# Attention: row minima and the two parts of the turned exponentials get a higher scheduling priority

## The chip, the cores and the metric

One core of a Trainium2 chip runs the whole program. The metric is the device time of one execution in microseconds (us). The engines are TensorE (PE in the profile; its weight loads are PEld), VectorE (DVE), ScalarE (ACT), GpSimd (POOL) and SyncE (SP, which issues DMAs). Each works off its own list of instructions in order; an instruction that has to wait holds everything behind it on that engine.

## The reference, cut to what matters

The model has two layers, each with a feed-forward part, a mixer and another feed-forward part, for 512 tokens of width 1024. The first mixer is a gated short convolution, the second is sparse attention. The change lies in the attention alone:

```python
def masked_softmax(logits, valid):
    p = jax.nn.softmax(jnp.where(valid, logits, NEG_INF), axis=-1)
    return jnp.where(valid, p, 0.0)
...
p_c = masked_softmax(s_c, dist_c >= 0)                 # 31 compressed blocks
p_s = masked_softmax(s_s, (dist_s >= 0)[:, :, None])   # selected blocks
p_w = masked_softmax(s_w, valid_w)                     # window
out = gb[..., 0:1] * o_c + gb[..., 1:2] * o_s + gb[..., 2:3] * o_w
```

There are 16 heads in 4 groups of 4; the heads of a group share keys and values. With 512 tokens all 8 selectable blocks are chosen, so the selected and the window branch are both plain causal attention over all tokens, each with keys of its own.

## The kernel before, in words

Matrix products are made from split values: a number is kept as a rounded high part and the low part that is left (`split`, L174: ScalarE copies the high part, VectorE subtracts it), and a product is three matmuls (`mm3`, L178).

`attend` (L1007) computes the attention. Its work comes in 32 **units**, one for each group g, head q of the group and branch b: units 0 to 7 are group 0, 8 to 15 group 1, and so on (L1010). The 512 query rows of a unit are four blocks of 128; block i sees (i+1)x128 keys. A unit is worked in three steps c, with the blocks (3), (2, 0) and (1). Per step and unit:

- `logits` (L1074): TensorE multiplies queries and keys into a PSUM tile `s` (L1084; two buffers). Queries and keys are held as a high and a low half in one tile, and the keys in both orders, so two matmuls make a block.
- `smallest` (L1089): VectorE adds the bias table, writes the (negated) logits to `L` and takes the minimum of each row in the same instruction (L1094); the second row that the order and the trace show for it reads the accumulator. There are four for a unit, one for each block. `L` has three buffers.
- `exponentials` (L1099): ScalarE takes the exponentials in place and sums the rows (L1103).
- `scaled` (L1106): when all four blocks are there, VectorE takes the reciprocal of the sums (L1109) and GpSimd multiplies it by the gate (L1111) and scales the four blocks of `L` (L1114).
- `turn` (L1116): TensorE transposes the blocks of `L` into a PSUM tile `pt` (L1123; two buffers). ScalarE copies the high part `pth` (L1127), VectorE subtracts it for the low part `ptl` (L1129, returned as `low` and called later).
- `apply` (L1131): TensorE multiplies values by `pth` and `ptl` into `o` (L1140, L1141); `finish` (L1143) adds the compressed branch from `pch`, `pcl` when a head is done, and VectorE and ScalarE write `osum`, `ohi`, `olo`.

The loop at L1209 is a software pipeline written by hand: with LEAD = 3, turn v brings `logits` and `smallest` of unit v+3, `scaled` of v+2, `turn` of v+1 and `apply` of v. Between these stand pieces of other work (`fill`): the projections of values and queries of later groups (`value_steps`, `query_steps`: 12 matmuls a piece into `nat`), a root-mean-square norm of the new queries on VectorE (`normed` L782, whose ten small instructions are `rsqrt` L202), their transposes into heads and keys (`heads` L993, `keys` L982), the compressed branch (`compressed` L1032: matmuls `pc`, VectorE rows L1045 to L1059, transposes `pct`), the output projection of finished groups (`out_steps` L1164: six matmuls into `y`, then `yt` on ScalarE and an addition on GpSimd), and weights for what follows, which VectorE and ScalarE split (`weights` L183; `wlo`, `ehlo` on VectorE). After the loop the tail multiplies the last two groups (`ty`, L1246).

The order in which instructions stand on each engine is not that of the text. A scheduler sets it: each instruction has a priority, by its place in the text unless `tc.high_priority()` raises it, and for each engine the scheduler takes, of what it reckons to be ready, what has the highest priority. The kernel already raises the norms between layers in this way (L266, L286, L382), nothing within `attend`. All other parts of the program are the same before and after.

Of the kernel before, what the change touches and what calls it, by code (L numbers as in the profile page):

```python
# [16 lines left out]
AF = mybir.ActivationFunctionType  # L17
# [36 lines left out]
def decoder_kernel(ctx, tc, xT, cT, ng, adaw, adab, ffi, ffo, cwi, cw, cwo,  # L54
                   nwi, nwg, pos, w1, w2, qg, kg, nwo, rb, onehot, rowok, out):
    nc = tc.nc
# [20 lines left out]
    def psum(name, tag="mm"):  # L77
        tag = next(six) if tag == "mm" else {"pr": "o"}.get(tag, tag)
        return ps.tile([P, T], F32, name=name, tag=tag, bufs=2)
# [650 lines left out]
    def nsa(s, nrm, nxt, w0, ahead):  # L730
        with ExitStack() as es:
# [112 lines left out]
            with ExitStack() as es2:  # L844
# [31 lines left out]
                run(v1[1:])  # L876
                keys(0, 1)
            return attend(es, s, nxt, ahead, K, Q, keys, heads, vn, kch, kcl, vcc, gsb, query_steps, value_steps, last_weight, hpool)


# [126 lines left out]
    def attend(nsa_es, s, nxt, ahead, K, Q, keys, heads, vn, kch, kcl, vcc, gsb, query_steps, value_steps, last_weight, hpool):  # L1007
# [3 lines left out]
        with ExitStack() as es:  # L1011
# [8 lines left out]
            def table(g, q):  # L1020
                n = g * NG + q
                for e in range(P // NR):
                    src = bass.AP(tensor=tbl.tensor, offset=tbl.offset + n * NR * TBL + P - 1 - NR * e,
                                  ap=[[TBL - 1, NR], [1, T]])
                    nc.sync.dma_start(tb[NR * e:NR * (e + 1), q, :], src)
# [48 lines left out]
            def logits(u, c):  # L1074
                g, q, b = units[u]
                if c == 0:
                    Ls[u] = at.tile([P, 1280], F32, name="L", bufs=3)
                    sts[u] = sp.tile([P, 2 * NB], F32, name="st")
                sps = psum("s", "s")
                off = 0  # L1080
                for i in ((3,), (2, 0), (1,))[c]:
                    n = (i + 1) * P
                    for e, m in enumerate(K[b]):
                        nc.tensor.matmul(sps[:, off:off + n], Q[q][:, i * P:(i + 1) * P], m[:, 0:n],  # L1084
                                         start=(e == 0), stop=(e == 1))
                    off += n
                return sps

            def smallest(u, c, sps):  # L1089
                g, q, b = units[u]  # L1090
                off = 0
                for i in ((3,), (2, 0), (1,))[c]:
                    n = (i + 1) * P
                    nc.vector.tensor_tensor_reduce(out=Ls[u][:, LOFF[i]:LOFF[i] + n], in0=sps[:, off:off + n],  # L1094
                                                   in1=tb[:, q, T - n:T], scale=1.0, scalar=3e38,
                                                   op0=ALU.add, op1=ALU.min, accum_out=sts[u][:, i:i + 1])
                    off += n

            def exponentials(u, c):  # L1099
                st = sts[u]  # L1100
                for i in ((3,), (2, 0), (1,))[c]:
                    l = Ls[u][:, LOFF[i]:LOFF[i] + (i + 1) * P]
                    nc.scalar.activation(l, l, AF.Exp, bias=st[:, i:i + 1], scale=-1.0,  # L1103
                                         accum_out=st[:, NB + i:NB + i + 1])

            def scaled(u):  # L1106
                g, q, b = units[u]
                r = sp.tile([P, NB], F32, name="r")
                nc.vector.reciprocal(r, sts[u][:, NB:2 * NB])  # L1109
                f = sp.tile([P, NB], F32, name="f")  # L1110
                nc.gpsimd.tensor_tensor(f, r, gsb[:, :, (g * 4 + q) * 3 + 2 - b], ALU.mult)  # L1111
                for i in range(NB):
                    l = Ls[u][:, LOFF[i]:LOFF[i] + (i + 1) * P]
                    nc.gpsimd.tensor_scalar(l, l, f[:, i:i + 1], 0.0, op0=ALU.mult, op1=ALU.add)  # L1114

            def turn(u, c):  # L1116
                pt = psum("pt", "t")
                off, segs = 0, []
                for j in ((0,), (1, 3), (2,))[c]:
                    segs.append((j, off))  # L1120
                    for i in range(j, NB):
                        cc = LOFF[i] + j * P
                        nc.tensor.transpose(pt[:, off:off + P], Ls[u][:, cc:cc + P], ident)  # L1123
                        off += P
                hi = at.tile([P, off], F32R, name=f"pth{c}")
                lo = at.tile([P, off], F32R, name=f"ptl{c}")
                nc.scalar.activation(hi, pt[:, 0:off], AF.Copy)  # L1127
                pts[u, c] = hi, lo, segs
                return lambda: nc.vector.tensor_tensor(lo, pt[:, 0:off], hi, ALU.subtract)  # L1129

            def apply(u, c):  # L1131
                g, q, b = units[u]
                hi, lo, segs = pts.pop((u, c))
                if b == 0 and c == 0:
                    os[g, q] = psum("o", "o")
                o = os[g, q]
                for j, cc in segs:
                    n = T - j * P
                    v = vn[b][j][:, g].rearrange("p a e -> p (a e)")
                    nc.tensor.matmul(o[:, j * P:T], v, hi[:, cc:cc + n], start=(b == 0 and j == 0), stop=False)  # L1140
                    nc.tensor.matmul(o[:, j * P:T], v, lo[:, cc:cc + n], start=False, stop=False)  # L1141

            def finish(u):  # L1143
                g, q, b = units[u]
                if b == 0:
                    return
                o = os.pop((g, q))
                nc.tensor.matmul(o, vz[:, q, :], pch, start=False, stop=False)
                nc.tensor.matmul(o, vz[:, q, :], pcl, start=False, stop=True)
                e = q % 2  # L1150
                if e == 0:
                    os["sum"] = at.tile([P, T], F32, name="osum")
                osum = os["sum"]
                mine, other = slice(e * HD, (e + 1) * HD), slice((1 - e) * HD, (2 - e) * HD)
                nc.scalar.activation(osum[mine], o[other], AF.Copy)
                nc.vector.tensor_tensor(osum[mine], o[mine], osum[mine], ALU.add)
                if e == 1:
                    hi, lo = [(tp if g % 2 else ow).tile([P, T], F32R, name=n, tag="t", bufs=4) for n in ("ohi", "olo")]
                    split(osum, hi, lo)
                    oh.append(hi)  # L1160
                    ol.append(lo)
# [17 lines left out]
            LEAD, N = 3, len(units)  # L1179
# [3 lines left out]
            for g in range(NG):  # L1183
                v0 = 8 * g
                c = compressed(g)
# [16 lines left out]
            def share(v):  # L1202
                for steps, v0, v1 in shares:
                    if v0 <= v < v1:
                        n = 11
                        return steps, n * (v - v0 + 1) // (v1 - v0) - n * (v - v0) // (v1 - v0), v == v1 - 1
                return None, 0, False

            for v in range(START, N):  # L1209
                a, b, u = v + LEAD, v + 1, v  # L1210
                steps, n, end = share(v)
                todo = needed[v] + [lambda: next(steps, None)] * n

                def fill(left):
                    for _ in range(-(-len(todo) // left)):
                        todo.pop(0)()

                for c in range(3):
                    if 0 <= u:
                        apply(u, c)  # L1220
                        if c == 2:
                            finish(u)
                    if 0 <= a < N:
                        sps = logits(a, c)
                    if c == 0 and 0 <= a - 1 < N:
                        scaled(a - 1)
                    if 0 <= b < N:
                        low = turn(b, c)
                    if 0 <= a < N:
                        smallest(a, c, sps)  # L1230
                    if 0 <= b < N:
                        low()
                    if 0 <= a < N:
                        exponentials(a, c)
                    fill(3 - c)
                for g, q in tables[v]:
                    table(g, q)
                if end:
                    for _ in steps:
                        pass  # L1240
# [121 lines left out]
```

## Time and profile before

| what | value |
|---|---|
| median of 3 runs | 1961.24 us |
| the three runs | 1961.24, 1954.09, 1961.82 us |
| the profiled execution's own time | 1954.91 us |
| its span, first to last instruction | 1952.8 us |
| mean granted TensorE clock | 0.997 of full speed |
| busy share: PE, PEld, DVE, ACT, POOL | 98%, 89%, 76%, 45%, 11% |

The profile is one execution, with times in microseconds from the start of the span. The attention loop runs from about 1345 to 1588. Rows of a view name an engine, a line of the kernel, the tile written and the tiles read. A matmul's duration holds its way through the array, so successive matmuls overlap; what one costs is the distance from one start to the next.

### The profile page before, as it was taken

To read this page: it belongs to the slowest core of one execution; us is meant where nothing else is said; L and a number is where in the kernel's file an instruction comes from. 1 tells how busy PE (TensorE), PEld (TensorE's weight loads), DVE (VectorE), ACT (ScalarE), POOL (GpSimd) and SP (SyncE) were. 2 spreads that over 40 slices of the span, in tenths; PEclk is the share of its full clock that TensorE was granted. 3 is DMA by queue.
4 is the path that set the end of the run, shared out by engine and by line. 5 is a ranking of instruction groups with operands and counts; after the bars stand their busy time and mean duration, and the time that the engine had idled before them with its cause. 6 is when DMAs were issued, how large, how long until landed. Compare 5 with 4: busy or idle time off the path is not lost.

```text
span 1952.8 us, 32447 instructions
## 1 busy us (share of the span) xinstructions
PE 1912.0 (98%) x12648; PEld 1732.9 (89%) x12648; DVE 1485.6 (76%) x2582; ACT 875.1 (45%) x1414; POOL 206.2 (11%) x281
## 2 busy tenths in 40 slices
PE   6999999999999999999999999999999899999999
PEld 4878888898899898999989999999888789898989
DVE  8878888674469586868968677886787879685965
ACT  3422223242236353435634343455777867353532
POOL 0000000100021000000000000001344630000000
PEclk9999999999999999999999999999999999999999
DMA  8898999523247564635646563143211224665622
GB/s 314 303 322 316 328 321 335 178 98 97 72 122 187 138 176 141 157 103 149 176 127 173 145 157 117 48 142 109 55 50 41 75 65 137 184 164 143 174 72 75
DMA packets 113110, 306.87 MB, mean 157 GB/s; under 512 B 13947, under 2 KB 14219, under 8 KB 112956
## 3 DMA queue, kind: packets, MB, share of 16 engines
q1 hardware_dynamic: 97308, 274.81, 42.0%
q0 software_dynamic: 15648, 29.99, 9.1%
q8 instruction: 99, 1.62, 0.3%
q14 instruction: 55, 0.45, 0.1%
HBM read 301.60 MB, written 3.15 MB: 156 GB/s over the span
## 4 chain that ended last, share of the span: by engine, by line
PE 77%; DVE 10%; DMA 7%; ACT 3%; issue 2%; SPq 1%; POOL 1%; DVEq 0%; ACTq 0%; POOLq 0%
PE gu L179 11%; PE gu L181 11%; PE gu L180 11%; DMA adaraw<-in_adaw 7%; PE y L179 6%; PE y L180 6%; PE y L181 6%; PE hs L181 2%; PE hs L180 2%; PE hs L179 2%; DVE adaraw L130 2%; DVE wlo L176 2%; PE cv L179 2%; PE cv L181 2%; PE cv L180 2%
## 5 line engine op out<-in xcount | busy, mean ns | idle before, releaser
L175 ACT ACTIVATE whi<-wraw 128x1024 fp32r<-128x1024 f32 (+2 forms) x283 | 281.9, 999 | 515.7 <-PE y L180 222.0
L176 DVE TENSOR_TENSOR wlo<-wraw,whi 128x1024 fp32r<-128x1024 f32 (+2 forms) x283 | 324.8, 1150 | 63.2 <-ACT whi L175 59.9
L179 PE MATMUL gu<-hhi,whi 128*128 128x256 f32 (+1 forms) x808 | 257.7, 319 | 0.0
L181 PE MATMUL gu<-hhi,wlo 128*128 128x256 f32 (+1 forms) x808 | 257.7, 319 | 0.0
L180 PE MATMUL gu<-hlo,whi 128*128 128x256 f32 (+1 forms) x808 | 257.6, 319 | 0.0
L179 PE MATMUL y<-ahi,whi 128*128 128x512 f32 x587 | 228.3, 391 | 0.5 <-ACT ahi L175 0.4
L180 PE MATMUL y<-alo,whi 128*128 128x512 f32 x587 | 227.5, 390 | 0.4 <-DVE alo L176 0.4
L181 PE MATMUL y<-ahi,wlo 128*128 128x512 f32 x587 | 227.0, 389 | 0.0
L130 DVE CUSTOM_DVE_ANT_0 adaraw<-adaraw,cond 128x1024 f32<-128x1024 f32 x144 | 174.7, 1222 | 34.8 <-DMA adaraw<-in_adaw 32.8
L180 PEld LDWEIGHTS gu<-hlo,whi 128*128 128x128 f32 x808 | 151.6, 188 | 12.3
L179 PEld LDWEIGHTS gu<-hhi,whi 128*128 128x128 f32 x808 | 151.7, 188 | 12.1
L181 PEld LDWEIGHTS gu<-hhi,wlo 128*128 128x128 f32 x808 | 151.7, 188 | 11.8
L528 POOL DMA_DIRECT2D qa<-in_ffi x54 | 65.0, 1204 | 738.5 <-DMA qa<-in_ffi 184.0
L179 PEld LDWEIGHTS y<-ahi,whi 128*128 128x128 f32 x587 | 109.5, 188 | 27.3 <-ACT ahi L175 4.7
L180 PEld LDWEIGHTS y<-alo,whi 128*128 128x128 f32 x587 | 110.2, 188 | 24.9 <-DVE alo L176 2.5
L181 PEld LDWEIGHTS y<-ahi,wlo 128*128 128x128 f32 x587 | 110.2, 188 | 22.6
L615 DVE SCALAR_TENSOR_TENSOR x<-y,mods,x 128x512 f32<-128x512 f32 x72 | 54.0, 750 | 98.4 <-PE y L181 98.3
L179 PE MATMUL gu<-th,qah 128*128 128x256 f32 x456 | 126.1, 276 | 0.0
L180 PE MATMUL gu<-tl,qah 128*128 128x256 f32 x456 | 125.9, 276 | 0.0
L180 PE MATMUL gu<-tl,qbh 128*128 128x256 f32 x456 | 125.9, 276 | 0.0
L181 PE MATMUL gu<-th,qbl 128*128 128x256 f32 x456 | 125.9, 276 | 0.0
L181 PE MATMUL gu<-th,qal 128*128 128x256 f32 x456 | 125.9, 276 | 0.0
(311 smaller groups left out, 5184.9 us busy)
## 6 DMA issues: line engine op xcount, KB each, us to landing
adaraw<-in_adaw SPq DMA_DIRECT2D x144, 512.0 KB, 6.0
wraw<-in_ffi SPq DMA_DIRECT2D x119, 512.0 KB, 4.1
qa<-in_ffi SPq DMA_DIRECT2D x114, 256.0 KB, 3.9
qa<-in_ffi POOLq DMA_DIRECT2D x54, 512.0 KB, 6.6
wraw<-in_ffo SPq DMA_DIRECT2D x72, 384.0 KB, 4.5
a<-in_ffi SPq DMA_DIRECT2D x57, 256.0 KB, 4.4
wraw<-in_cwi SPq DMA_DIRECT2D x24, 512.0 KB, 3.3
wraw<-in_nwi SPq DMA_DIRECT2D x20, 512.0 KB, 3.6
```

What stands on the lines that cost most here:

```text
L130: nc.vector.tensor_tensor_reduce(out=raw, in0=raw, in1=cond, scale=1.0, scalar=0.0, op0=ALU.mult, op1=ALU.add, accum_out=m)
L175: nc.scalar.activation(hi, src, AF.Copy)
L176: nc.vector.tensor_tensor(lo, src, hi, ALU.subtract)
L179: nc.tensor.matmul(o, sh, mh, start=first, stop=False)
L180: nc.tensor.matmul(o, sh, ml, start=False, stop=False)
L181: nc.tensor.matmul(o, sl, mh, start=False, stop=last)
L528: nc.gpsimd.dma_start(qa, bass.AP(tensor=a21.tensor, offset=a21.offset, ap=[a21.ap[0], [0, 2], a21.ap[1]]), accum_op=ALU.add)
L615: nc.vector.scalar_tensor_tensor(x[d], o, mod(s, 2, d), x[d], op0=ALU.mult, op1=ALU.add)
```

## The change

Three things get `tc.high_priority()`: the row minima (L1094), the high part of the turned exponentials on ScalarE (L1127), and its low part on VectorE (L1129). Nothing is added, removed or computed differently. The lines below move down by one to three in the changed file: L1129 becomes L1130, L1156 becomes L1157.

```diff
                 hi = at.tile([P, off], F32R, name=f"pth{c}")
                 lo = at.tile([P, off], F32R, name=f"ptl{c}")
-                nc.scalar.activation(hi, pt[:, 0:off], AF.Copy)
+                with tc.high_priority():
+                    nc.scalar.activation(hi, pt[:, 0:off], AF.Copy)
                 pts[u, c] = hi, lo, segs
                 return lambda: nc.vector.tensor_tensor(lo, pt[:, 0:off], hi, ALU.subtract)
...
                     if 0 <= b < N:
                         low = turn(b, c)
-                    if 0 <= a < N:
-                        smallest(a, c, sps)
-                    if 0 <= b < N:
-                        low()
+
+                    with tc.high_priority():
+                        if 0 <= a < N:
+                            smallest(a, c, sps)
+                        if 0 <= b < N:
+                            low()
                     if 0 <= a < N:
                         exponentials(a, c)
```

The same instructions stand on every engine in another order, in the attention and just behind it. Three places follow; numbers behind a name tell buffers apart, and are the same before and after.

**Place A, VectorE, end of group 0.** From the first to the second low part of unit 4 (`ptl0_14197`, `ptl1_14226`); `L_14178` is unit 6, `L_14272` unit 7. The row that reads the accumulator behind each minimum is left out here. Before:

```order
L1129 TENSOR_TENSOR ptl0_14197<-pt_14191,pth0_14196 128x512
L213 TENSOR_TENSOR rs_b_14145<-rs_a_14144,vq_13741 128x16
L1094 ISA L_14178,st_14179<-s_14215,tb_13504 128x384
L214 SCALAR_TENSOR_TENSOR rs_r0_14146<-rs_b_14145,rs_j_14142 128x16
L1094 ISA L_14178,st_14179<-s_14215,tb_13504 128x128
L217 TENSOR_TENSOR rs_a_14150<-rs_r0_14146 128x16
L218 TENSOR_SCALAR rs_r1_14152<-rs_r0_14146 128x16
L1129 TENSOR_TENSOR ptl1_14226<-pt_14220,pth1_14225 128x512
```

And changed:

```order
L1130 TENSOR_TENSOR ptl0_14197<-pt_14191,pth0_14196 128x512
L783 TENSOR_SCALAR vq_13741<-vq_13741 128x16
L1109 RECIPROCAL r_14277<-st_14179 128x4
L176 TENSOR_TENSOR wlo_14862<-wraw_14863,whi_14861 128x1024
L1094 ISA L_14272,st_14273<-s_14274,tb_13504 128x512
L1094 ISA L_14272,st_14273<-s_14309,tb_13504 128x384
L1094 ISA L_14272,st_14273<-s_14335,tb_13504 128x256
L1130 TENSOR_TENSOR ptl2_14256<-pt_14252,pth2_14255 128x256
L1094 ISA L_14272,st_14273<-s_14309,tb_13504 128x128
L1130 TENSOR_TENSOR ptl1_14226<-pt_14220,pth1_14225 128x512
```

The minima of unit 7 have moved ahead of the second low part of unit 4, and the norm of the next group's queries (rows L207 to L221) from here to behind it.

**Place B, VectorE, end of group 2.** The last rows of the norm of group 3's queries (`qn30`, `qn31`). Before, with low parts of units 20 and 21 (`ptl2_15942`, `ptl0_15977`) between them:

```order
L219 TENSOR_TENSOR rs_b_15851<-rs_a_15850,vq_15490 128x16
L1129 TENSOR_TENSOR ptl2_15942<-pt_15938,pth2_15941 128x256
L220 SCALAR_TENSOR_TENSOR rs_a_15853<-rs_b_15851 128x16
L1109 RECIPROCAL r_15963<-st_15865 128x4
L1129 TENSOR_TENSOR ptl0_15977<-pt_15971,pth0_15976 128x512
L221 SCALAR_TENSOR_TENSOR rs_r2_15854<-rs_a_15853,rs_r1_15852 128x16
L176 TENSOR_TENSOR olo_15932<-osum_15725,ohi_15931 128x512
L787 TENSOR_TENSOR qn30_15488<-qn30_15488,rs_r2_15854 128x512
L787 TENSOR_TENSOR qn31_15489<-qn31_15489,rs_r2_15854 128x512
```

And changed, with the low parts of unit 23 (`ptl0_16160`, `ptl2_16222`, `ptl1_16189`), the last of the group:

```order
L219 TENSOR_TENSOR rs_b_15851<-rs_a_15850,vq_15490 128x16
L1130 TENSOR_TENSOR ptl0_16160<-pt_16154,pth0_16159 128x512
L220 SCALAR_TENSOR_TENSOR rs_a_15853<-rs_b_15851 128x16
L176 TENSOR_TENSOR wlo_16846<-wraw_16847,whi_16845 128x1024
L1130 TENSOR_TENSOR ptl2_16222<-pt_16218,pth2_16221 128x256
L1130 TENSOR_TENSOR ptl1_16189<-pt_16183,pth1_16188 128x512
L221 SCALAR_TENSOR_TENSOR rs_r2_15854<-rs_a_15853,rs_r1_15852 128x16
L787 TENSOR_TENSOR qn30_15488<-qn30_15488,rs_r2_15854 128x512
L787 TENSOR_TENSOR qn31_15489<-qn31_15489,rs_r2_15854 128x512
```

The queries of group 3 are normed behind all of group 2; before they were ready while units 22 and 23 had still to be turned. TensorE's list follows: the first logits of group 3 (`s_16038`, unit 24) stood before between the second and third transposes of unit 22, and stand now behind the last product of unit 23.

**Place C, TensorE, the last units.** The transposes of group 3's compressed branch (`pct`) and the output projection of group 1 behind them (`y_16407`; three more pieces of six follow). Before they stand at unit 25, between logits of unit 27 (`s_16416`) and transposes of unit 25 (`pt_16419`):

```order
L1084 MATMUL s_16416<-k11_12320,q1_12322 128x256
L1064 MATMUL pct_16374<-ident_106,pcs_13505 128x128 x4
L179 MATMUL y_16407<-ohi_15079,whi_16341 128x512
L180 MATMUL y_16407<-olo_15080,whi_16341 128x512
L181 MATMUL y_16407<-ohi_15079,wlo_16342 128x512
L179 MATMUL y_16407<-ohi_15510,whi_16341 128x512
L180 MATMUL y_16407<-olo_15511,whi_16341 128x512
L181 MATMUL y_16407<-ohi_15510,wlo_16342 128x512
L1123 MATMUL pt_16419<-ident_106,L_16141 128x128 x2
```

And changed, behind pieces of the tail (`ty`) and behind the last logits of unit 31:

```order
L181 MATMUL ty_16913<-ohi_16322,ehlo_16465 128x256
L1064 MATMUL pct_16374<-ident_106,pcs_13505 128x128 x4
L179 MATMUL y_16407<-ohi_15079,whi_16341 128x512
L180 MATMUL y_16407<-olo_15080,whi_16341 128x512
L181 MATMUL y_16407<-ohi_15079,wlo_16342 128x512
L179 MATMUL y_16407<-ohi_15510,whi_16341 128x512
L180 MATMUL y_16407<-olo_15511,whi_16341 128x512
L181 MATMUL y_16407<-ohi_15510,wlo_16342 128x512
L1149 MATMUL o_16347<-pch_13508,vz_13506 128x512
```

All 24 `y` matmuls of this half have left units 25 to 28 for the end; units 24 to 27 are finished (`o_16347`) only there.

## Rows read from the trace of the kernel before

**Rows 1.** Stretches of the attention: busy time by engine, clock, DMA share, GB/s.
```profile
core 0: us, PE busy (x) PEld busy (x) DVE busy (x) ACT busy (x) POOL busy (x), PEclk, DMA share, GB/s
1381.00:1425.00 44.00, 39.98 (x285) 36.41 (x285) 34.13 (x98) 32.95 (x83) 16.58 (x37) 0.96 0.20 55
1517.50:1530.20 12.70, 10.34 (x58) 7.59 (x58) 12.30 (x36) 12.03 (x31) 5.26 (x8) 1.00 0.24 63
...
1544.90:1587.10 42.20, 40.05 (x258) 34.09 (x257) 35.10 (x98) 34.55 (x87) 24.48 (x40) 1.00 0.08 26
1340.00:1600.00 260.00, 243.19 (x1681) 217.21 (x1679) 203.51 (x561) 193.34 (x470) 118.28 (x203) 0.99 0.23 61
```
**Rows 2.** Waits, 1340 to 1600: who waited for whom, us in total, times, longest.
```profile
PEld s L1084 <- DVE st L1094: 5.0, 8, 1.2
PEld pt L1123 <- DVE ptl L1129: 4.4, 10, 0.8
PE pt L1123 <- DVE ptl L1129: 4.2, 8, 0.9
```
**Rows 3.** Groups of instructions, 1348 to 1590: busy us, mean ns | idle before.
```profile
L1114 POOL TENSOR_SCALAR L<-L,f 128x128 f32<-128x128 f32 (+3 forms) x128 | 72.2, 583 | 3.1
L1103 ACT ACTIVATE L<-L,st 128x512 f32<-128x512 f32 (+3 forms) x128 | 71.0, 556 | 9.3 <-DVE st L1094 8.6
L1094 DVE CUSTOM_DVE_ANT_0 L<-s,tb 128x512 f32<-128x512 f32 (+3 forms) x128 | 59.9, 481 | 22.9 <-PE s L1084 10.6 <-PE pt L1123 9.0 <-DMA tb<-tbl 2.6
L1129 DVE TENSOR_TENSOR ptl<-pt,pth 128x512 fp32r<-128x512 f32 (+1 forms) x96 | 57.1, 595 | 9.3 <-ACT pth L1127 8.4
L1127 ACT ACTIVATE pth<-pt 128x512 fp32r<-128x512 f32 (+1 forms) x96 | 49.9, 523 | 29.2 <-PE pt L1123 28.3
L1103 ACT ACTIVATION_READ_ACCUMULATOR L<-L,st 128x1 f32 x128 | 24.4, 191 | 0.0
L176 DVE TENSOR_TENSOR wlo<-wraw,whi 128x1024 fp32r<-128x1024 f32 x12 | 16.2, 1353 | 3.8 <-ACT whi L175 3.8
L1156 DVE TENSOR_TENSOR osum<-o,osum 64x512 f32<-64x512 f32 x16 | 11.0, 687 | 2.5 <-ACT osum L1155 2.2
L1094 DVE DVE_READ_ACCUMULATOR2_ANT st<- 128x1 f32 x128 | 10.3, 80 | 0.0
L176 DVE TENSOR_TENSOR ehlo<-wraw,ehhi 128x1024 fp32r<-128x1024 f32 x4 | 4.9, 1217 | 0.3 <-ACT ehhi L175 0.3
L787 DVE TENSOR_TENSOR qn<-qn,rs_r 128x512 f32<-128x512 f32 x6 | 4.1, 714 | 0.0
L214 DVE SCALAR_TENSOR_TENSOR rs_r<-rs_b,rs_j 128x16 f32<-128x16 f32 x3 | 1.5, 485 | 0.0
L221 DVE SCALAR_TENSOR_TENSOR rs_r<-rs_a,rs_r 128x16 f32<-128x16 f32 x3 | 0.5, 163 | 0.0
```
**Rows 4.** Timeline at place B: start us, us, engine, line, operation.
```profile
1516.16 0.51 DVE L207 TENSOR_SCALAR rs_i<-vq 128x16 int32<-128x16 int32 x1
1522.72 1.48 DVE L787 TENSOR_TENSOR qn<-qn,rs_r 128x512 f32<-128x512 f32 x2
1527.57 0.50 PE L1084 MATMUL s<-k,q 128*128 128x512 f32 x1 [0.38 <-ACT k L988]
```
**Rows 5.** Chain of waits, 1405 to 1412: start us, us, what ran.
```profile
1406.97 0.47 PE s L1084 x2
1408.51 0.57 PE s L1084 x4
1409.08 0.46 PE pt L1123 x4
```
**Rows 6.** Timeline of TensorE: first logits of unit 28 and of unit 31.
```profile
1560.05 0.62 PE L1084 MATMUL s<-k,q 128*128 128x512 f32 x2
1574.92 0.68 PE L1084 MATMUL s<-k,q 128*128 128x512 f32 x2
```
**Rows 7.** A stretch at a lower clock, columns as in rows 1.
```profile
1421.00:1425.00 4.00, 4.00 (x20) 3.91 (x20) 1.04 (x4) 0.87 (x3) 1.74 (x5) 0.57 0.00 0
```
**Rows 8.** The last of 16 narrow matmuls just before it, in the timeline.
```profile
1420.88 0.26 PE L1039 MATMUL pc<-kcl,q 128*128 128x32 f32 x1
```

## The prediction

> **What bounds the kernel now.** I read the attention's stretches first. In the 260 us around the loop TensorE is busy for 243.2, VectorE for 203.5 and ScalarE for 193.3 (78% and 74%) [rows 1]. TensorE sets the end and stands idle for 16.8 us; no better order can bring more than that, as long as TensorE's work stays what it is. Second, the waits: TensorE and its weight loads wait for row minima (they give back a buffer of `s`) and for low parts (they give back a buffer of `pt`), 5.0 + 4.4 + 4.2 = 13.6 us in all [rows 2]. These are the waits that the change aims at. Third, the groups of instructions, for what a unit costs on each engine [rows 3]. ScalarE: four exponentials and their accumulator reads, 4 x (0.556 + 0.191), and three high parts, 3 x 0.523, together 4.56 us. VectorE: 4 x (0.481 + 0.080) for minima and 3 x 0.595 for low parts, 4.03 us. TensorE by distances between starts [rows 5]: the logits are two matmuls of width 512 (0.47), four of widths 384 and 128 (0.57) and two of width 256 (0.24, half of 0.47 by my estimate), 1.28 us; the transposes 0.46 + 0.46 + 0.23 = 1.15; the products have the logits' widths, some 1.28; in all 3.7 us. So the units by themselves run at the pace of ScalarE, not of TensorE: at the end of the loop, where few other pieces stand between them, units 28 to 31 start (1574.92 - 1560.05)/3 = 4.96 us apart [rows 6]. The loop's mean is 243/32 = 7.6 us a unit, since TensorE has filler pieces between. **The fillers keep TensorE busy; without one, a unit leaves 4.6 - 3.7 = 0.9 to 4.96 - 3.7 = 1.3 us of TensorE idle.** The question is whether the fillers still stand where they are needed.
>
> **Part 1, the steady middle.** Inside a group the minima and low parts already stand near the head of VectorE's list, and TensorE's order is nearly kept. Of the 13.6 us some may go. What displaces them: both have the same raised priority, so at place A minima go ahead of a low part that TensorE waits for. I take -1 us; the ends are -13.6 (every such wait goes) and 0 (they change places).
>
> Here a page speaks for more. By TensorE's matmul row only 16.8 of 260 us are free, by its weight loads 260 - 217.2 = 42.8 us [rows 1]. The Trainium skill, page "Perfetto Trace Analysis", section Identifying the Most-Contended Engine, says that matmul busy time misjudges the headroom since matmuls are pipelined, and that the weight loads' busy share tells it better; by it up to 42.8 us could be had, and the gain here would have a lower end of -42.8. I stay with 16.8: starts 0.46 us apart for four transposes show no gap that a VectorE order would close [rows 5].
>
> **Part 2, place A (end of group 0).** Means of rows 3 overstate a stretch, since neighbours overlap. From L207 to the end of the `qn` pair at place B the list of before holds 9.55 us by these means and took 1522.72 + 1.48 - 1516.16 = 8.04 us [rows 4], a factor of 0.84, which I use on VectorE. Between the first and second low part of unit 4 stood two minima and five small norm rows (0.16 to 0.49, some 1.1 us): 2 x 0.561 + 1.1 = 2.2, x 0.84 = 1.9 us. Now stand there four minima, `wlo` 1.35, a low part 0.60, a reciprocal and a small row (0.2 each, estimated from L221): 2.24 + 1.35 + 0.60 + 0.4 = 4.6, x 0.84 = 3.8 us [rows 3]. `pt` has two buffers, so transposes of unit 5 wait behind it: 3.8 - 1.9 = +1.9. The queries of group 1, normed later, cost little: 48 matmuls of projections follow the first logits of unit 8 in TensorE's new list and can cover their way through softmax. With two like places I take **+2.5**, ends 0 (fillers cover the wait) and +4.
>
> **Part 3, place B (end of group 2).** This is the largest term. The queries of group 3 are normed only behind unit 23. From the first low part of unit 20 to `qn31` VectorE now has: 7 minima 3.93, 11 low parts 6.55, ten norm rows 2.5, 2 `osum` 1.37, `olo` 0.73 (an addition of like shape, estimated from `qn`), 3 `ehlo` 3.65, `wlo` 1.35, two `qn` 1.43 and small ones 0.7: 22.2 us, x 0.84 = 18.7 against 8.04 before, that is 10.6 us later [rows 3, 4]. The first logits of unit 24, at 1527.57 before [rows 4], wait for these queries through their transposes and heads. TensorE first has work brought forward: transposes of units 22 and 23, products of 22 and 23 and the closing products of a head, 0.23 + 1.15 + 2 x 1.28 + about 0.35 = 4.3 us. Left: 10.6 - 4.3 = 6.3 us of idle. Then the pipeline fills anew: unit 24 must pass minima, exponentials, reciprocal, gate and scaling (4 x 0.583 on GpSimd) before its first transposes, and only 18 `y` matmuls and the next logits stand between; I charge +1.2. Sum **+7.5**; ends 0 (fillers cover all) and 10.6 + 1.2 = +12. In the trace of before the same stretch lost little: TensorE busy 10.34 of 12.70 us [rows 1].
>
> **Part 4, place C (group 3).** The compressed transposes `pct` and 24 `y` matmuls leave units 25 to 28 and stand behind the last logits; 24 x 0.235 = 5.6 us of filler is gone from there (half of 0.47 again, [rows 5]). From the transposes of unit 25 to the logits of unit 31 some 4.5 units now run at 4.6 and not at TensorE's 3.7: 4.5 x 0.9 = 4 us. Since `o` has two buffers and the heads of units 24 to 27 are finished only when `pct` is there, products of unit 28 wait too, some 0.8; against that stands what was idle there before, 42.20 - 40.05 = 2.15 us, of which I take half as lost already [rows 1]. **+4**; ends 0 and 4.5 x 1.3 + 0.8 = +6.7. The moved matmuls run densely afterwards and cost what they cost before.
>
> **The sum.** -1 + 2.5 + 7.5 + 4 = **+13 us** on the profiled execution's 1954.9, that is 1968. The median of the runs, 1961.2, lies 6.3 above that execution, between runs of 1954.1 and 1961.8, so the same sum gives 1974 on the median; I name **1971**. No DMA is added, and DMA engines are busy for 23% here [rows 1]; the rest of the program is the same.
>
> **The rivals.**
> *The fillers cover it (no change).* The pieces behind the first logits of units 8 and 24 and the work brought forward keep TensorE busy, so that part 3 falls to +2.5 and the others to +3 together, less some of the waits: 0 to +6, 1958 to 1967. For it: VectorE is idle for 56 of 260 us and may catch up faster than a list by means says. Against: at place B it was busy for 12.30 of 12.70 us [rows 1]. It decides whether unit 24's first logits start less than 4 us after the last product of unit 23.
> *The waits vanish (faster).* Minima and low parts come earlier at every unit, 13.6 us [rows 2] mostly go, and VectorE's own idle time hides the late norm: -6 to -13, 1948 to 1955. It decides where the late norm costs under 3 us; then the waits saved win. Against it: the order hardly changes in the middle, where most of these waits lie, and a single late norm at place B takes half of it back.
> *The clock falls in the gaps (slower still).* In the trace of before the granted clock stood at 0.57 over 4 us [rows 7], the 1.2 GHz level for most of it; before it, TensorE ran 16 narrow products of the compressed branch [rows 8]. Such a fall costs (1 - 0.57) x 4 = 1.7 us. With several gaps of some us at places A, B and C and three or four falls, +13 becomes +20 or more, 1975 to 1990. The Trainium skill, page "TensorE: Matmul & The Clock Gate", Part 1, says that the clock falls back when the array is idle; the rows show one fall without an idle stretch, and a fall behind an idle one is not shown in this stretch.
> *The change does nothing* can be set aside: the order moves at all three places.
>
> **The numbers.** About 0.5% (9.8 us) is what a measurement of this kernel can tell from no change. Forecast (+8 to +20): 0.47, of which 0.05 fall below +9.8. Clock falls as well: 0.10, all slower. Cover: 0.31, all within. Waits vanish: 0.12, of which 0.08 beyond -9.8. That gives slower 0.42 + 0.10 = 0.52, the same 0.05 + 0.31 + 0.04 = 0.40, faster 0.08. The range leaves out the fast end of the last case and the far end of the clock's: 1954 to 1986. The likeliest case alone spans 1966 to 1981.
>
> **What would show it.** Right: the attention loop, 243 us before, grows by about 13, and the growth sits in three places: TensorE idle near the end of group 0, some 6 us of idle between the last product of unit 23 and the first logits of unit 24, with a wait for `qn` or the heads made of it, and start distances near 4.6 to 5 us from unit 25 to 31 with TensorE partly idle, then a dense run of `y`. Waits for minima and low parts in the middle should shrink a little. Wrong: no idle stretch at place B; or a loop that grows evenly, which would mean that low parts behind minima, not the late norm, carry the cost; or a loop that is shorter, with the waits of rows 2 gone.

## The result and the profile after

The changed kernel takes 1983.72 us (median of 6 runs, 1979.71 to 1987.24), the kernel before 1960.88 (6 runs): 22.8 us more, ratio 1.0131 with the interval [1.0115, 1.0148]. The direction was forecast; the size, +10 on the median and +13 on the profiled execution, was about half of what came (+22.8 and +24.8).

The profiled execution of the changed kernel took 1979.71 us, the shortest of its six runs; its span is 1977.9. For where the time went I take the **loop distance**: from the start of the first logits (L1084) to the start of the last matmul of L272, the first norm behind the loop. It is 1612.81 - 1343.45 = 269.36 us before and 1637.95 - 1344.17 = 293.78 after. The difference, 24.4 us, is nearly all of the 25.1 by which the spans differ. Windows of the kernel before, the loop distance and a stretch at a lower clock (columns as in [rows 1]):

```profile
1343.45:1612.81 269.36, 251.79 (x1748) 225.16 (x1745) 213.91 (x597) 197.25 (x482) 118.24 (x203) 0.99 0.22 60
1366.00:1370.00 4.00, 4.00 (x24) 4.00 (x23) 1.68 (x6) 1.57 (x5) 0.00 (x0) 0.57 0.00 0
```

And of the changed kernel, the loop distance, three stretches at a lower clock, the end of group 2 and group 3:

```profile
1344.17:1637.95 293.78, 265.47 (x1748) 230.96 (x1745) 215.93 (x597) 198.04 (x482) 114.46 (x203) 0.97 0.20 55
1430.00:1441.00 11.00, 11.00 (x55) 10.87 (x54) 3.88 (x12) 2.06 (x6) 1.96 (x4) 0.53 0.06 12
1542.00:1546.00 4.00, 3.97 (x18) 2.99 (x18) 3.35 (x7) 2.17 (x4) 2.82 (x5) 0.58 0.00 0
1556.00:1560.00 4.00, 4.00 (x15) 3.27 (x14) 2.70 (x5) 2.87 (x6) 1.69 (x2) 0.57 0.00 0
...
1535.00:1555.00 20.00, 13.55 (x70) 9.63 (x70) 15.48 (x35) 12.30 (x26) 7.46 (x13) 0.91 0.34 106
1561.00:1590.00 29.00, 27.19 (x178) 23.08 (x176) 22.74 (x75) 23.79 (x68) 16.77 (x31) 1.00 0.06 20
```

Both loops hold the same 1748 matmuls. TensorE is idle for 17.6 us before and 28.3 after, and its busy time grew too, by 13.7, though it does the same work. Half of that growth is the clock. A fall costs (1 - 0.57) x 4 = 1.7 us of full speed; before there are two (1366 and [rows 7]), 3.4 us; after there is one at 1365 (0.57 over 4 us) and the three shown, 1.7 + 11 x (1 - 0.53) + 1.7 + 1.7 = 10.2 us. The clock takes 6.8 us more; the other 17.6 are the order's: 10.7 of idle, and 6.9 of matmuls held up while they count as busy. These 6.9 sit in the transposes into `pt` for the most part, whose 320 matmuls are busy for 58.8 us and were for 53.2 (a part of this is the clock's).

Waits of the changed kernel, who waited for whom, beside [rows 2]:

```profile
PEld pt L1123 <- POOL L L1114: 14.6, 28, 1.1
...
PE pt L1123 <- POOL L L1114: 6.3, 15, 0.9
PEld s L1084 <- DVE st L1094: 5.8, 11, 1.3
PE pt L1123 <- DVE ptl L1130: 4.6, 10, 1.1
...
PEld pt L1123 <- DVE ptl L1130: 3.4, 10, 0.6
```

The waits at which the change aimed are still there: 5.8 + 4.6 + 3.4 = 13.8 us against 13.6. Another has grown far beyond them: transposes wait 14.6 + 6.3 = 20.9 us for GpSimd's scaled blocks. Before, it was 2.9 + 0.6 = 3.5:

```profile
PEld pt L1123 <- POOL L L1114: 2.9, 6, 1.1
...
PE pt L1123 <- POOL L L1114: 0.6, 1, 0.6
```

The rows of PEld count waits of weight loads, which run beside matmuls still in flight (the busy times of the two, 265.47 and 230.96 us, share 293.78); so these sums say who is waited for, and are not idle time, of which TensorE has 28.3 us in all.

GpSimd is no busier than before (114.46 us for 118.24); it waits for the reciprocal. Timeline of the changed kernel in group 1, one unit:

```profile
1473.03 0.51 ACT L1103 ACTIVATE L<-L,st 128x256 f32<-128x256 f32 x1
...
1478.86 0.17 DVE L1109 RECIPROCAL r<-st 128x4 f32<-128x4 f32 x1
...
1480.38 0.20 POOL L1111 TENSOR_TENSOR f<-r,gsb 128x4 f32<-128x4 f32 x1
1480.68 1.39 POOL L1114 TENSOR_SCALAR L<-L,f 128x128 f32<-128x128 f32 x3
...
1481.11 0.33 PE L1123 MATMUL pt<-ident,L 128*128 128x128 f32 x1 [0.36 <-POOL L L1114]
```

The unit's last exponentials end at 1473.54, and 0.17 us of work that they free starts 5.3 us later, behind raised minima and low parts for the most part (1.4 us are `osum` and `olo`). From the end of a unit's last exponentials to its reciprocal the 32 units take 0.53 us on average before and 2.08 after.

Timeline of the changed kernel at place B:

```profile
1549.93 0.17 DVE L221 SCALAR_TENSOR_TENSOR rs_r<-rs_a,rs_r 128x16 f32<-128x16 f32 x1
...
1550.13 1.29 DVE L787 TENSOR_TENSOR qn<-qn,rs_r 128x512 f32<-128x512 f32 x2
...
1550.69 0.28 PE L1142 MATMUL o<-ptl,vn 128*128 128x256 f32 x1
...
1550.88 0.44 PE L979 MATMUL pq<-ident,qn 128*128 128x128 f32 x2
...
1551.96 1.38 ACT L998 ACTIVATE q<-pq,qgs 64x512 fp32r<-64x512 f32 x2 [3.18 <-PE pq L979]
...
1554.05 0.68 ACT L988 ACTIVATE k<-pk,kgs 64x512 fp32r<-64x512 f32 x1
...
1554.79 0.30 PEld L1084 LDWEIGHTS s<-k,q 128*128 128x128 f32 x2 [2.72 <-ACT k L988]
1554.79 0.50 PE L1084 MATMUL s<-k,q 128*128 128x512 f32 x1 [2.29 <-ACT k L988]
```

The queries of group 3 are ready at 1551.42, before at 1524.20 [rows 4]; the first logits of group 3 at 1554.79 wait for their heads and keys. From 1535 to 1555 TensorE is idle for 20 - 13.55 = 6.45 us, and its clock falls twice near the end of group 2, at 1542 and at 1556. Only 2.29 us of that idle time lie between the last product of unit 23, which ends at 1550.97, and these logits.

### The profile page after: what moved, and what is told of

Read it like the earlier page. It is cut to its first block, busy times and chain, and to the rows that moved or that the text cites. A ratio compares the mean times of both kernels' runs of the same rounds, so it can differ in the third digit from the quotient of the medians.

```text
span 1977.9 us, 32445 instructions
## 1 busy us (share of the span) xinstructions
PE 1926.3 (97%) x12648; PEld 1738.9 (88%) x12648; DVE 1487.8 (75%) x2582; ACT 875.4 (44%) x1414; POOL 202.5 (10%) x281
## 4 chain that ended last, share of the span: by engine, by line
PE 82%; DVE 8%; DMA 3%; issue 2%; ACT 2%; POOL 1%; SPq 1%; DVEq 0%; POOLq 0%; ACTq 0%
PE gu L179 12%; PE gu L181 12%; PE gu L180 12%; PE y L179 7%; PE y L180 7%; PE y L181 7%; DMA adaraw<-in_adaw 2%; PE hs L180 2%; PE hs L181 2%; PE hs L179 2%; PE cv L180 2%; PE cv L181 2%; PE cv L179 2%; PE ty L180 2%; PE ty L181 2%
## 5 line engine op out<-in xcount | busy, mean ns | idle before, releaser
L181 PEld LDWEIGHTS gu<-hhi,wlo 128*128 128x128 f32 x808 | 151.7, 188 | 11.9
L181 PEld LDWEIGHTS y<-ahi,wlo 128*128 128x128 f32 x587 | 110.6, 188 | 22.8
L179 PE MATMUL gu<-th,qbh 128*128 128x256 f32 x456 | 125.9, 276 | 0.0
```

The lines of the kernel that those rows point to most:

```text
L179: nc.tensor.matmul(o, sh, mh, start=first, stop=False)
L181: nc.tensor.matmul(o, sl, mh, start=False, stop=last)
```

## The experiments

Theory 1: what is left at normal priority on VectorE (reciprocals, the norm of the next queries) falls behind raised work and starves TensorE. Theory 2: raised minima displace the low parts. Later the clock came in as a cause by itself. All runs in one table. "Loop" is the loop distance of the profiled execution less 269.4; "clock" is what its falls cost, summed over stretches of 1 us as 1 less the granted clock; "order" is the loop's difference less the clock's (clock - 3.4). A single execution can lie off its median, so the last column does the same with every run: each run's time less its span times (1 less its mean granted clock), averaged, against the same of the kernel before. A mean clock is on record for every run but those of the kernel before beside the change, for which the mean of the other comparisons, 1950.8, stands in. The 95% intervals of this column reach 1 to 3.3 us to either side.

That a fall costs what is charged for it shows in the kernel before itself: its 23 runs beside e17 go from 1951.08 us at a clock of 1.000 to 1968.41 at 0.992, with 1.03 us of time for each us so charged; less that, their range shrinks from 17.3 to 8.1 us. Its order is the same in all of them, so most of this spread is the clock's.

| run | median, against before, us | ratio, 95% interval | loop | clock | order | order, all runs |
|---|---|---|---|---|---|---|
| the change | +22.8 | 1.0131 [1.0115, 1.0148] | +24.4 | 10.2 | +17.6 | +16.5 |
| e1 minima | +8.3 | 1.0041 [1.0024, 1.0059] | +7.7 | 8.5 | +2.6 | +5.7 |
| e2 high and low parts | +13.2 | 1.0067 [1.0039, 1.0095] | +14.2 | 10.2 | +7.4 | +8.9 |
| e3 high parts | -2.8 | 0.9985 [0.9970, 1.0001] | -3.9 | 1.7 | -2.2 | -1.9 |
| e4 low parts | +15.0 | 1.0075 [1.0045, 1.0104] | +16.9 | 11.9 | +8.4 | +9.0 |
| e5 group 0 | +8.3 | 1.0032 [1.0009, 1.0054] | +11.7 | 10.2 | +4.9 | +5.6 |
| e6 group 1 | -0.2 | 0.9996 [0.9982, 1.0009] | +3.2 | 3.4 | +3.2 | +2.9 |
| e7 group 2 | +8.2 | 1.0038 [1.0021, 1.0054] | +8.2 | 3.4 | +8.2 | +8.0 |
| e8 group 3 | +1.3 | 1.0007 [0.9991, 1.0023] | +8.6 | 10.2 | +1.8 | +3.3 |
| e9 change + reciprocal | +20.4 | 1.0097 [1.0076, 1.0118] | +20.9 | 13.6 | +10.7 | +10.7 |
| e10 change, not turns 19-23 | +16.1 | 1.0080 [1.0051, 1.0110] | +18.3 | 10.2 | +11.5 | +12.0 |
| e11 groups 0 and 1 | +14.5 | 1.0067 [1.0046, 1.0088] | +18.9 | 13.7 | +8.6 | +9.9 |
| e12 high parts + reciprocal | +0.6 | 0.9994 [0.9979, 1.0009] | +6.7 | 13.7 | -3.6 | -1.5 |
| e13 change, not 3-7, 19-23 | +12.4 | 1.0064 [1.0044, 1.0084] | +11.8 | 6.8 | +8.4 | +8.8 |
| e14 e11 + reciprocal | +7.9 | 1.0044 [1.0024, 1.0063] | +9.4 | 8.5 | +4.3 | +5.2 |
| e15 high parts + norm | -7.4 | 0.9967 [0.9952, 0.9982] | -7.2 | 1.7 | -5.5 | -4.4 |
| e16 e15 + compressed | +0.5 | 1.0001 [0.9986, 1.0015] | +4.3 | 11.9 | -4.2 | -4.6 |
| e17 e15, one block | +1.3 | 1.0005 [0.9989, 1.0021] | +0.5 | 10.2 | -6.3 | -6.3 |
| e18 e15, small blocks | -7.6 | 0.9962 [0.9943, 0.9980] | -5.1 | 3.4 | -5.1 | -4.6 |

**By part (e1 to e4).** Of the change, only the named `tc.high_priority()` stays; e1:

```diff
-                    with tc.high_priority():
-                        if 0 <= a < N:
-                            smallest(a, c, sps)
-                        if 0 <= b < N:
-                            low()
+                    if 0 <= a < N:
+                        with tc.high_priority():
+                            smallest(a, c, sps)
+                    if 0 <= b < N:
+                        low()
...
-                with tc.high_priority():
-                    nc.scalar.activation(hi, pt[:, 0:off], AF.Copy)
+                nc.scalar.activation(hi, pt[:, 0:off], AF.Copy)
```

> Only the row minima are raised; high and low parts have the priority of before. Theory 1 (what is left at normal priority on VectorE, the reciprocals and the query norm, falls behind the raised work): half of the raised VectorE work is there, the first logits of unit 24 stand behind the first transposes of unit 23 and not behind the last product of unit 23; +6 to +12 us over the kernel before. Theory 2 (low parts stand behind raised minima and the transposes wait for them): minima alone do it all, low parts now lose every contest: +20 or more, with the waits of transposes for low parts grown to over 15 us.

> Only the high and low parts are raised; the minima have the priority of before. Theory 1: the other half of the raised work, with the first logits of unit 24 behind the second product of unit 22: +6 to +12 us. Theory 2: without raised minima nothing stands ahead of a low part, -5 to 0 us.

> Only the high parts on ScalarE are raised. Theory 1: VectorE's list is not pushed by it; the first logits of unit 24 stand where they stood; within 3 us of the kernel before. A rival by which ScalarE's exponentials, pushed back by high parts, are the loss: +8 or more.

> Only the low parts on VectorE are raised. Theory 1: reciprocals and the norm fall behind low parts alone: +2 to +7 us. Theory 2: -5 to 0 us.

Theory 2 falls: raised minima alone cost 8.3 us and not 20, and low parts raised alone, with nothing ahead of them, cost 15.0 and not less than nothing. Theory 1 held for e1 and e3; e2 and e4 cost more than it said (13.2 for at most 12, 15.0 for at most 7). ScalarE's part costs nothing and may gain. The harm is done by the two raised things on VectorE, each by itself.

For low parts alone Theory 1 has the sign but not the way. In e4 the reciprocal starts 0.66 us after its unit's last exponentials (0.49 in e2, 0.53 before, 1.60 in e1), and the first logits of unit 24 stand almost where they stood. Still the transposes wait 18.9 us for scaled blocks:

```profile
PEld pt L1123 <- POOL L L1114: 12.3, 19, 1.4
...
PE pt L1123 <- POOL L L1114: 6.6, 12, 1.2
```

From a unit's last logits to its last scaled block e4 takes 7.18 us on average, before 6.43; 0.33 of the difference lie at the minima, which now stand behind raised low parts, and 0.20 at the exponentials. TensorE's list has also drawn closer: 53.6 matmuls stand between a unit's last logits and its first transposes, before 58.2. Which of the two makes the cost no run shows. In the whole change the minima are raised too and end earlier (0.94 us after their unit's last logits, before 1.75), and there it is the reciprocals that are late.

**By place (e5 to e8).** Raised in the turns of one group alone (`v` is the loop's turn):

```diff
+            def raised(v):
+                return tc.high_priority() if v < 8 else nullcontext()
...
-                with tc.high_priority():
+                with raised(u - 1):
...
-                    with tc.high_priority():
+                    with raised(v):
```

> All three are raised in the turns of the loop before group 1 alone (turns up to 7), the rest is as before. The trace of the change lost some 8 us up to the logits of unit 10, with part of it at half clock; by the theory of late reciprocals and a late norm at each group's end this returns alone: +5 to +9 us. If a group's loss comes only from what piles up over the whole loop: within 2 us.

> Raised in turns 8 to 15 alone. By the prediction's part 1 the middle gains or stays, -2 to 0 us. By the theory of late reciprocals (in the trace of the change the reciprocal starts 2.4 us after the last exponential of its unit in group 1, 0.5 before) it costs +3 to +7 us here.

> Raised in turns 16 to 23 alone; the first logits of unit 24 stand behind the last product of unit 23, as with the whole change. By the prediction's part 3 +7.5 us, with part of part 4 in it; by the trace of the change +8 to +12, and the clock falls behind the gap.

> Raised in turns 24 to 31 alone; the queries of group 3 are normed as early as before, and the compressed transposes come at unit 29. By the prediction's part 4 +4 us; by the trace of the change, which loses nothing on balance behind unit 25, -2 to +1.

Groups 0 and 2 cost as expected. For group 1 the median shows nothing, as the prediction's part 1 would have it; the order costs +3.2 in the profile and +2.9 over all runs, at the low end of what late reciprocals were expected to cost, and runs that lost less to the clock than those of the kernel before (6.7 us for 9.3) hid it. Group 3 costs +1.8 by the profile and +3.3 over all runs. The order column adds up: 4.9 + 3.2 + 8.2 + 1.8 = 18.1, the whole change 17.6; over all runs it is 19.8 for 16.5, within the intervals. The medians do not (+17.6 against +22.8): the changed kernel's runs lose 16.5 us each to the clock, those of e5 to e8 between 6.7 and 11.3. The profile of e8 shows how a fall can come without a cause in the order. Up to unit 24 its lists are those of the kernel before, and yet its clock fell where that kernel's did not:

```profile
1489.00:1500.00 11.00, 11.00 (x54) 10.81 (x54) 6.19 (x21) 5.02 (x15) 2.26 (x5) 0.54 0.11 21
```

That is 5.1 us in one stretch; this execution took 1970.95 us, its kernel's median is 1960.87. The clock's falls differ between executions of one kernel.

**Undoing causes (e9 to e14).** e9 adds to the change:

```diff
-                nc.vector.reciprocal(r, sts[u][:, NB:2 * NB])
+                with tc.high_priority():
+                    nc.vector.reciprocal(r, sts[u][:, NB:2 * NB])
```

> The whole change, and the reciprocal of the row sums raised as well, so that it stands behind its unit's last exponentials at once. Theory of late reciprocals: the waits of transposes for scaled blocks (20.9 us in the trace of the change, 2.9 before) fall below 8 us and 6 to 10 us of the loss come back: +13 to +18 us over the kernel before. Theory that the late query norms and what follows a gap carry the loss: the norm is still behind unit 23, +20 us or more, and the waits only change their name.

e10 and e11 use `raised` with `not 19 <= v < 24` and `v < 16`; e12 is e3 with the raised reciprocal, e13 has `not (3 <= v < 8 or 19 <= v < 24)`, e14 is e11 with the raised reciprocal.

> The whole change but for turns 19 to 23, the end of group 2: the queries of group 3 are normed early again and the first logits of unit 24 stand behind the second product of unit 21. By the run with group 2 alone (+8 us) the time is +14 to +17 us over the kernel before; no gap of over 2 us before the logits of unit 24. By a theory in which the loss of a late norm is only moved elsewhere: still +20 or more.

> Raised in turns up to 15 alone. If the regions add up (+8 and 0 us by their runs alone): +6 to +10 us. If group 1 pays because group 0 leaves it late (in the trace of the change it lost 6 us more there): +12 to +16 us.

> A try at a faster kernel: only the high parts and the reciprocals are raised, the low parts and minima are as before. Both short items, so by the theory that long raised work on VectorE does the harm nothing is pushed back: -8 to -2 us against the kernel before. A rival by which any raised instruction on VectorE delays the norm: 0 or more.

> The whole change but for turns 3 to 7 and 19 to 23, the ends of groups 0 and 2. If the late query norms at the ends start nearly all of it (gap, clock, and a pipeline that is late in the group behind): 0 to +7 us over the kernel before. If raised minima and low parts cost by themselves in each group: +10 or more.

> Turns up to 15 raised, and the reciprocals raised throughout. The run without the reciprocals was +13 us. If late reciprocals are how group 1 pays for a late start: +6 to +9 us, with the waits for scaled blocks under 7 us. If it is the clock or the order of TensorE alone: +11 or more.

The end of group 2 is worth 22.8 - 16.1 = 6.7 us by the medians (e10, as expected), 6.1 by the order column and 4.5 by all runs. Groups 0 and 1 together cost 14.5 by the median, as expected if group 1 pays for a late start; but their order, +8.6 and +9.9, is no more than that of the two alone (4.9 + 3.2 and 5.6 + 2.9), and the rest is the clock's. With the reciprocal raised the transposes' waits in e9 are

```profile
PEld pt L1124 <- POOL L L1115: 6.6, 12, 1.4
...
PE pt L1124 <- POOL L L1115: 3.4, 7, 1.2
```

10.0 us for 20.9, and the order column gives 6.9 back (17.6 to 10.7), all runs 5.8 (16.5 to 10.7). In e14 the wait fell from 12.2 + 4.5 in e11 to

```profile
PEld pt L1127 <- POOL L L1115: 2.5, 5, 1.1
...
PE pt L1127 <- POOL L L1115: 0.7, 1, 0.7
```

and the order column from 8.6 to 4.3, all runs from 9.9 to 5.2. The medians give 2.4 and 6.6 us, with intervals that overlap. By its median, +20.4, and by waits that stayed above 8 us, e9 falls to its second theory; its order says otherwise, and its clock, 13.6 us in the profile and 18.3 over all runs, took the gain. Part of the waits did change their name: those for low parts are 11.9 us in e9, 8.0 in the change. e13 decided against the theory that the ends start nearly all: with both undone +12.4 are left, +8.4 of it order. e12 missed: its order is 3.6 us better by the profile and 1.5 over all runs, which its interval does not tell from nothing, and its clock ate that. The whole change with the query norm raised beside it was not run, so what the late norm alone costs is not shown.

**The cause turned round (e15 to e18).** e15 keeps the raised high part, takes minima and low parts back, and raises the query norm's chain:

```diff
+                    with tc.high_priority():
+                        nc.scalar.activation(sq, o, AF.Square)
...
+                    def close():
+                        with tc.high_priority():
+                            normed(dst, v)
+                    return raw(dst, v), close
...
+                    needed[v0 - 5].append(lambda g=g: first(heads, g, 0))
...
+                    needed[v0 - 2].append(lambda g=g: first(heads, g, 1))
```

`first` calls its argument under `tc.high_priority()`, and so it does with the steps of `compressed` in e16. e17 and e18 change e15 only in where `compressed` yields between its 32 narrow matmuls (L1039), and with it in the turns that ask for its steps: e17 never yields, e18 after each block of rows but the last.

> The high parts raised, and with them the queries' squares, norm, transposes into heads and their evictions; minima and low parts as before. The first logits of unit 24 stand behind the third transposes of unit 21, earlier than in the kernel before. If early norms do the reverse of late ones: -3 to -8 us against the kernel before. If the norm was early enough and hidden already: within 3 us.

> As the run before, and the compressed branch's steps raised too, so that its transposes stand some two units earlier. If the finishes of heads wait for it: 1 to 4 us below the run before; if it is hidden: the same, or above it where its five long additions push minima back.

> The kernel of e15 (7.4 us faster than before) with the 32 narrow products of a group's compressed branch in one block and not in two of 16; the order is else nearly the same. If such a block drops the clock: at half clock in three or four groups, 1.7 to 3.4 us each, and +4 to +10 us over e15, so -3 to +3 us against the kernel before. If e16 lost its time by the raised steps of the compressed branch: within 2 us of e15, -9 to -5.

> The kernel of e15 with the products given out block row by block row; in TensorE's list they stand in blocks of 8, 8 and 16 in three of the four groups. If the block's length drops the clock: as e15 or up to 2 us faster, the clock fallen at most twice. If the clock has nothing to do with it: within 2 us of e15.

e15 is faster than both kernels. Windows of its loop and of its one fall:

```profile
1345.01:1607.12 262.11, 247.78 (x1747) 222.91 (x1745) 212.23 (x597) 196.28 (x482) 116.69 (x203) 0.99 0.22 61
1521.00:1526.00 5.00, 4.07 (x14) 3.28 (x15) 3.37 (x10) 4.06 (x10) 1.42 (x3) 0.66 0.07 20
```

TensorE is idle for 14.3 us, 3.2 less than before. Of the 7.4 us some 3 are the high parts' (e3), and the rest comes with the norm; the norm was not raised by itself, and the intervals of e3 and e15 overlap. e16 missed: expected below e15, it gave all back, to the clock (11.9), with an order as good as e15's (-4.6 and -4.4 over all runs). There the 32 narrow products stand in one block in three of the four groups, and the clock falls in the middle of these blocks. Two windows of e16, 8 us before such a fall and the 8 us that hold it:

```profile
1474.00:1482.00 8.00, 8.00 (x54) 6.96 (x53) 5.61 (x16) 7.60 (x16) 5.60 (x7) 1.00 0.06 10
1482.00:1490.00 8.00, 8.00 (x41) 7.92 (x41) 5.39 (x14) 2.29 (x5) 3.15 (x5) 0.57 0.20 66
```

TensorE is busy for all of both; the products run from 1480.1 to 1484.7. e17 does little but put the products in one block (27, 32, 28 and 32 of them without a break) and costs 8.6 us over e15 (1959.51 against 1950.95), of which the clock column explains 10.2 - 1.7 = 8.5. At the end of its third block:

```profile
1484.00:1491.00 7.00, 7.00 (x32) 6.96 (x32) 4.09 (x12) 2.10 (x6) 0.93 (x2) 0.51 0.37 103
```

e18, with smaller blocks, is as e15, which both of its expectations allow; it decides nothing between them.

## Why the prediction was right or wrong

**What bounds it:** right. TensorE sets the end, and its idle time grew by 10.7 us because work that feeds it came late.

**Part 1, the middle, -1 us: wrong in sign, and the largest miss.** "Of the 13.6 us some may go": none went, they changed places. The step that failed is to look only at the waits that the change aimed at, and not at what the raised work displaces inside a group. The reciprocal, which part 2 counts as a small row of 0.2 us, was not followed to who waits for it: it came 2.08 us after its unit's exponentials and not 0.53, and the waits for scaled blocks went from 3.5 to 20.9 us. Raising it gives back 5.8 to 6.9 us of order (e9). Group 1 raised alone costs +3.2 and +2.9 in order, and with both ends undone +8.4 are left (e13), of which group 3 makes 2 to 3; the middle so costs some 5 to 7 us (an estimate from e13 less e8), where -1 was forecast. The headroom of 42.8 us by the weight loads, told beside this part, was not drawn on.

**Part 2, the end of group 0, +2.5: right in sign, half in size, and partly by luck.** The order costs +4.9 by the profile of e5 and +5.6 over all runs. The way forecast, transposes of unit 5 behind a late low part, is not what grew: waits for low parts are 9.7 us in e5 for 8.6 before, those of the logits for row minima 12.8 for 7.3, those for scaled blocks 6.8 for 3.5. (Before, four small norm rows stand between the two low parts and not five; the sum moves by less than 0.2 us.)

**Part 3, the end of group 2, +7.5: right in size.** e7 measures +8.2 both ways, e10 takes 4.5 to 6.7 back. Its norm was forecast 10.6 us late; it came 27.2 late, of which the loop was behind already by 15.3 (the first logits of unit 20 start at 1514.27, before at 1498.93): 11.9. The forecast's 6.3 us of idle did not come as one gap. TensorE is idle for 6.45 us in 20, where the 20 us up to the same logits held 2.78 before, and only 2.29 lie between the last product of unit 23 and the first logits of unit 24: TensorE had been waiting before the norm was done.

**Part 4, group 3, +4: the size is not excluded, the reason is wrong.** Raised alone it costs +1.8 by the profile and +3.3 over all runs, and the median, +1.3, has an interval of about -1.8 to +4.5. The pace was as forecast, (1590.26 - 1560.98)/6 = 4.9 us a unit from unit 25 to 31, but TensorE is busy there for 27.19 of 29 us: narrow products and pieces of the tail stood between, more than the 3.7 us that were counted, so the reason given for the pace, an idle TensorE, is not what came.

**The sum:** the order costs 17.6 and not 13 by the profile, 16.5 by all runs; what is missing lies in parts 1 and 2. The clock costs 6.8 more in the profile, and over all runs the changed kernel loses 16.5 us to it where the kernel before loses 7.3 to 9.3. The prediction kept this out of the sum, as a rival of 0.10 at "+20 or more" that would come in the forecast's place; it came beside the forecast. So two steps failed: the middle's term has the wrong sign, and the clock's term was put at nothing. The named 1971 is also 3 us below the 1974 that the prediction's own sum gives on the median.

**The rivals:** the fillers did not cover, though the sign named for it, first logits of unit 24 less than 4 us after the last product of unit 23, was met (3.8 us): most of the idle time lay earlier. The waits did not vanish. As for the clock, two of the falls stand behind idle time, at 1542 and 1556, and two around narrow products, at 1365 and 1430. The base held: the profiled execution of before, at 3.4 us of clock in the loop, lies 6 us below its kernel's median.

## What to carry to other kernels

In this kernel raising a link of a chain pushed back the links left at normal priority. It paid to raise the short work that others wait for (a norm's chain, a high part), and it cost to raise the long work of which there is always more (minima, low parts); e15 against e4 is 22 us of difference. Follow each small instruction to who waits for it before pricing it by its length. And when TensorE is the bound, look at the granted clock of each stretch, and of each run before comparing medians: a better order can be lost to it, as in e16.

## What the runs showed of the hardware that was not expected

TensorE's clock fell to the 1.2 GHz level not only behind gaps but around narrow matmuls (128x32) with the engine busy throughout the fall: 5.1 us lost in one stretch in the changed kernel and in e8, 3.4 us in each of three of e16's and two of e17's. The Trainium skill, page "TensorE: Matmul & The Clock Gate", Part 1, ties the lower level to an idle array. The windows of e16 show a fall without idleness in this row, 8.00 of 8 us busy on both sides of it; others, as the one at 1556 in the changed kernel, do stand behind idle time (2.29 us, from 1552.50 to 1554.79). The same products in two blocks of 16 a group cost none in e15, but in the kernel before, with such blocks too, both falls stand right behind one (at 1366, and at 1421 [rows 8]). Whether a fall comes varies from execution to execution with the same lists: the kernel before ran at mean clocks from 0.992 to 1.000. Which property of the narrow products counts was not tried.
